# Layer 0 of a two-layer block: an interleaved opening, adaLN pieces of four k-tiles used two units behind their load, five granules, and the mixer's gate summed on PE

## The chip, the cores and the metric

The kernel runs on one core of a Trainium2 chip. The metric is the device time of one execution in microseconds. A core has five engines with an instruction stream of their own each: PE (matrix products), DVE and ACT (elementwise work), POOL (small work, and DMA issues of its own) and SP (which here only issues DMAs). Each stream is executed in order. Sixteen DMA engines carry all transfers.

## What is computed

Two layers over 256 tokens of width 2048, all in float32. Layer 0 has differential attention as its mixer, layer 1 a state-space mixer, and each has a gated feed-forward network (FFN). Cut to what matters here:

```python
c_act = jax.nn.silu(c)                              # 1 x 2048
for i in range(2):
    ada = c_act @ ada_w[i] + ada_b[i]               # 2048 x 12288
    shift1, scale1, gate1, shift2, scale2, gate2 = split(ada, 6)
    h = rms_norm(x, norm1_g[i]) * (1.0 + scale1) + shift1
    m = diff_attention(h, ...) if i == 0 else mamba2_ssd(h, ...)
    x = x + gate1 * m
    h = rms_norm(x, norm2_g[i]) * (1.0 + scale2) + shift2
    x = x + gate2 * swiglu(h, ffn_w_gate_up[i], ffn_w_down[i])
```

The adaLN vectors are products of one row with a large matrix: for layer 0 each of the six chunks is 2048 x 2048 weights, 16.8 MB, that are read once.

## The kernel before

**Weights and units.** Every weight matrix is read once, in units of 256 rows x 512 columns (0.524 MB), into a buffer `raw` of the pool `rawp` (seven buffers). ACT rounds it to `wh` (L268), DVE takes the rest `wl` (helper line L126), and PE multiplies: per unit two k-tiles x two token blocks x three products (`wh` by `ah`, `wl` by `ah`, `wh` by `al`), that is 12 products of 512 columns. Layer 0's input projection `da_w_in` is 96 units (12 blocks of columns, 8 units deep, the tuple `(n, half)`), its output projection `da_w_out` 32 units.

**The order of the work** is set when the program is written out. `push_unit` loads a unit and puts its products into a list, `fifo`; a unit's products are written when four more units have been pushed, so PE works four units behind the loads. `tick()`, once for each unit of products, also steps the generators of attention and lets adaLN jobs out at `ada["rate"]` jobs a unit.

**adaLN of layer 0** is computed in two ways. Shift and scale of the mixer come in *granules* of columns (`GRANULES`, six of them), laid out on the host by `lay_mods` as pieces of 128 partitions x 1024 (0.524 MB). A piece is used on PE: four products at a time with `cT32` (silu(c), each value repeated 32 times), in four column groups of the array, into bank `po` (shift) or `wk` (scale). `push_raw` puts a piece's use into the same `fifo`, so it comes up to four units behind its load. When a vector of a granule is done, ACT copies the sums (`adasb`), PE adds the four groups with `c32`, DVE makes `T0` and `S0`, and `modulate` makes the factors `ah`, `al` of these columns. The other vectors (mixer's gate `m0`, FFN's shift and scale `f0`) are *jobs* (`ada_job`): one row tile of 128 x 1024 is loaded and added up on DVE (`acc`). Shift and scale end in products with `ones` on PE, the gate in `partition_all_reduce` on POOL. The gate has 34 jobs, two of them for the bias.

**The opening.** `turn_x` takes the squares of x (ACT), `rstd` (POOL), scales x and turns it on PE into `xT`. The pieces of granule 0 follow. The small columns (`Columns`: norm gains and biases) and the rotary inputs come in through POOL's own queue; the buffer of `Columns` is one of `rawp`, and the rotary inputs lie in its rest.

**The input projection** goes through `order`: first every block's half 0, then deeper ones as granules become ready; partial sums that must leave PE's banks are put aside (`put_aside`, ACT copy or DVE addition). When a block of q or k is complete, its epilogue (normalising, rotary, transposes) runs as a generator, and behind it 12 attention steps (`attend`: four groups of heads x three), started at least four ticks apart. `until_output(g)` and `flush_steps` force the steps on when the output projection needs heads that are not there yet. `add_sums(ch)` adds a block of output to x with the gate; ahead of it `flush_jobs` writes out all jobs but the last 17, or all.

Of the kernel before, what the change touches and what calls it, by code (L numbers as in the profile page):

```python
# [20 lines left out]
D = 2048  # L21
# [24 lines left out]
GRANULES = [(0, 256), (256, 256), (512, 256), (768, 512), (1280, 512), (1792, 256)]  # L46
# [32 lines left out]
def lay_mods(w):  # L79

    import numpy as np

    parts = []
    for f, n in GRANULES:
        a = 1024 // n
        for v in range(2):
            m = w[:, v * D + f:v * D + f + n]
            parts.append(m.reshape(-1, a, 128, n).transpose(0, 2, 1, 3).reshape(-1))
    return np.ascontiguousarray(np.concatenate(parts)[None, :])
# [13 lines left out]
def block_kernel(ctx: ExitStack, tc: tile.TileContext, x, c, positions, norm1_g, norm2_g, ada_w, ada_b,  # L103
# [61 lines left out]
    waiting = {"u": 0, "a": 0}  # L165
    limit = {"u": W_BUFS, "a": 4}
# [42 lines left out]

    def tick():  # L210
# [12 lines left out]
        step_all()  # L223
# [60 lines left out]

    def push_raw(ap, fn):
# [4 lines left out]
        sp.dma_start(raw, ap)  # L290
        waiting["a"] += 1
        fifo.append(("a", lambda: fn(raw)))
# [86 lines left out]
    class Columns:  # L379


        def __init__(self, groups):

            self.groups = groups
            self.st = rawp.tile([128, 8, 128], F32, tag="raw", name="stage")
            for i, (_, aps) in enumerate(groups):
                r = 0
                for a in aps:
                    pool.dma_start(self.st[r:r + a.shape[0], i, :], a)
                    r += a.shape[0]  # L390

        def finish(self, i):
# [15 lines left out]
                     (bias_cols[1], [bias_rows[1, v:v + 2].rearrange("v k p -> (v k) p") for v in (0, 3)])])  # L408
    ps = bank("wk")
    pe.transpose(ps[:, :16], crows, ident[:16, :16])  # L410
    cT = const.tile([128, 16], F32, name="cT")
    act.activation(cT, ps[:, :16], AF.Silu)
# [277 lines left out]
    dp = pha.enter_context(tc.tile_pool(name="dp", bufs=1))  # L690
    cT32 = dp.tile([128, 512], F32, tag="on", name="cT32", bufs=1).rearrange("p (k m) -> p k m", m=32)
    dve.tensor_copy(cT32, cT[:, :, None].to_broadcast([128, 16, 32]))

    for b in range(2):
        sp.dma_start(xt[b], x[0, b * 128:(b + 1) * 128, :])
# [9 lines left out]
    lv = cols0.st[:, 4:6, :].rearrange("p a (i d) -> p (a i) d", d=64)  # L705
# [83 lines left out]
    def turn_x():  # L789

        junk = rowp.tile([128, D], F32, tag="gate", name="junk")
        rx = []
        for b in range(2):
            s = small(1, "ssum")
            act.activation(junk, xt[b], AF.Square, accum_out=s)
            rx.append(rstd_of(s, 1, D, "rstd"))
        for q in range(4):
            for b in range(2):
                xn = tmp("xn")
                if b:  # L800
                    dve.tensor_scalar(xn, xq[b][q], rx[b], None, op0=ALU.mult)
                else:
                    act.mul(xn, xq[b][q], rx[b])
                ps = bank("wk")
                for i in range(4):
                    pe.transpose(ps[:, i * 128:(i + 1) * 128], xn[:, i * 128:(i + 1) * 128], ident)
                dst = xT[q][:, :, b * 128:(b + 1) * 128]
                src = ps.rearrange("p (k t) -> p k t", k=4)
                if b:
                    act.copy(dst, src)  # L810
                else:
                    dve.tensor_copy(dst, src)

    def modulate(gi):

        f, n = GRANULES[gi]
        for k in range(f // 128, (f + n) // 128, 2):
# [11 lines left out]
            dve.tensor_tensor(l[:, k2, :], hm, h[:, k2, :].bitcast(F32), op=ALU.subtract)  # L829

    def granule(gi):

        f, n = GRANULES[gi]
        per = 1024 // n
        count = 16 // per
        sl = slice(f // 128, (f + n) // 128)
        nk = n // 128
        items = []

        def one(vec):  # L840
            st = {"held": []}

            def use(raw, u):
                if u == 0:
                    st["ps"] = bank(("po", "wk")[vec])
                st["held"] += [(u * per + a, raw[:, a * n:(a + 1) * n]) for a in range(per)]
                if len(st["held"]) < 4:
                    return
                for k, w in st["held"]:
                    g = k % 4  # L850
                    pe.matmul(st["ps"][32 * g:32 * g + 32, :n], cT32[:, k, :], w, start=(k < 4),
                              stop=(k >= 12), tile_position=(0, 32 * g), skip_group_check=True)
                st["held"] = []
                if u == count - 1:
                    st["sb"] = tmp("adasb")
                    act.copy(st["sb"][:, :n], st["ps"][:, :n])

            def finish():
# [8 lines left out]
            def push(u):  # L867
                at = f * 4096 + vec * n * D + u * 131072
                ap = bass.AP(tensor=ada_m.tensor, offset=ada_m.offset + at, ap=[[1024, 128], [1, 1024]])
                push_raw(ap, lambda raw: use(raw, u))  # L870
            for u in range(count):
                items.append(lambda u=u: push(u))
            return finish
        ends = [one(0), one(1)]
        return items, ends

# [191 lines left out]
    def put_aside(n):  # L1068

        bk = hold.pop(n)()  # L1070
# [12 lines left out]
    def push_step(n, half, first, last):  # L1083
# [5 lines left out]
        def run(u):  # L1089
            for b in range(2):  # L1090
                products(bk()[b], hq[q][b], half % 2, u, 512, first, last)
        push_unit(wi, half * 256, i * D + hg * 512, 512, run)
        if last:
            call(lambda: put_aside(n))

    split_at = 8
    order = [(n, 0) for n in range(split_at - 1, -1, -1)] + [(n, 0) for n in range(split_at, 12)]
    order += [(11, 1), (10, 1), (11, 2), (10, 2)]
    order += [(n, h) for n in range(9, split_at - 1, -1) for h in (1, 2)]
    order += [(n, h) for n in range(split_at - 2) for h in (1, 2)]  # L1100
    order += [(n, h) for n in (split_at - 2, split_at - 1) for h in (1, 2)]
    order += [(n, h) for n in range(split_at - 1, -1, -1) for h in (3, 4)]
    order += [(n, h) for n in range(split_at) for h in (5, 6, 7)]
    order += [(n, h) for n in range(split_at, 12) for h in (3, 4, 5, 6, 7)]
# [9 lines left out]

    made = [granule(gi) for gi in range(len(GRANULES))]

    def done_with(gi, vec):
        made[gi][1][vec]()
        if vec:
            modulate(gi)  # L1120

    turn_x()
    for k, it in enumerate(made[0][0]):
        it()
        if k == 5:
            def small_columns():
                for k in range(3):
                    cols0.finish(k)
                dve.tensor_scalar(subc, gcols[:, 64:65], 1.0 - LAMBDA_INIT, None, op0=ALU.mult)
            call(small_columns)  # L1130
# [5 lines left out]
    for gi in range(1, len(GRANULES)):  # L1136
        items = made[gi][0]
        for k, it in enumerate(items):
            ends = [(gi, k // (len(items) // 2))] if (k + 1) % (len(items) // 2) == 0 else []
            todo.append((it, ends))  # L1140
    late = deque()

    def ada_items(n):
        while late:
            call(late.popleft())
        for _ in range(n):
            if todo:
                it, ends = todo.popleft()
                it()
                for e in ends:  # L1150
                    late.append(lambda e=e: done_with(*e))

    call(lambda: done_with(0, 0))
    call(lambda: done_with(0, 1))
    open_ = set()
    pace = 0.0
    for at, (n, half) in enumerate(order):
        pace += 4 / 3 if at < 12 else 8 / 7
        ada_items(int(pace))
        pace -= int(pace)  # L1160
        if at == 16:
            call(lambda: active.append(rotary_tables()))
        if not todo and not late and not ada["rate"]:
            call(lambda: ada.update(rate=1.4))
            ada["rate"] = 1e-9
# [27 lines left out]
    def add_sums(ch):  # L1193
        flush_jobs(0 if ch == 2 else 17)
# [157 lines left out]
    def ssd_load():  # L1352
# [3 lines left out]
                                        ssd_ng[0].rearrange("(k p) -> k p", p=128)])])  # L1356
# [401 lines left out]
```

## Time and profile before

| | |
|---|---|
| median of 3 runs | 2791.36 us (2790.69 to 2792.46) |
| the profiled execution | 2787.28 us, span 2785.6 us |
| PE busy | 2665.7 us, 96% |
| DVE, ACT, POOL busy | 1936.5, 1314.9, 255.0 us |
| mean DMA rate | 246 GB/s |

Times in the profile count from the start of the span. A row of the timeline has start, length, engine, line, operation, output and inputs, and in brackets the idle time before it and what ended it. A fp32 product stands in the trace as two records, so counts there are double those of the program. Matrix products overlap in the pipeline, so their busy time isn't the time that each adds; that is read from the starts of neighbouring rows.

### The profile page before, as it was taken

How to read it: one execution, taken by the hardware profiler on the slowest of the kernel's cores; microseconds unless marked ns; L12 is line 12 of the kernel's file. 1: busy time of each engine (PE TensorE's matmuls, PEld its weight loads, DVE VectorE, ACT ScalarE, POOL GpSimd, SP SyncE). 2: the span in 40 equal slices, each digit the busy share in tenths (PEclk: the TensorE clock that was granted, in tenths of full speed). 3: DMA queues.
4: the chain of work that ended last, by engine and by line, in shares of the span. 5: the costliest groups of instructions: out<-in, count | busy, mean ns of one | idle time of the engine just before them, and what ended most of it. 6: DMA issues, size and time to landing. Idle time of an engine off the chain costs nothing.

```text
span 2785.6 us, 35877 instructions
## 1 busy us (share of the span) xinstructions
PE 2665.7 (96%) x13333; PEld 2207.0 (79%) x13333; DVE 1936.5 (70%) x2204; ACT 1314.9 (47%) x1844; POOL 255.0 (9%) x254
## 2 busy tenths in 40 slices
PE   3999889779999999999999999999999999999999
PEld 2666667658888888888899899888888888888887
DVE  1356999678878888677777877877664444445776
ACT  2433456445444444444655566564554444444443
POOL 2000424210211111000100001001000000000001
PEclk8999999889999999999999999999999999999999
DMA  4788877668899998788456666666645555556885
GB/s 167 264 306 296 284 272 266 235 240 289 316 336 353 338 330 318 260 289 296 147 193 219 224 226 216 236 218 211 220 155 188 194 189 190 189 188 211 292 289 184
DMA packets 188942, 684.56 MB, mean 246 GB/s; under 512 B 22224, under 2 KB 22528, under 8 KB 187488
## 3 DMA queue, kind: packets, MB, share of 16 engines
q1 hardware_dynamic: 186160, 678.59, 69.6%
q0 software_dynamic: 2176, 3.60, 0.4%
q8 instruction: 104, 1.70, 0.2%
q14 instruction: 70, 0.57, 0.1%
q10 hardware_dynamic: 432, 0.10, 0.0%
HBM read 680.00 MB, written 2.20 MB: 245 GB/s over the span
## 4 chain that ended last, share of the span: by engine, by line
PE 81%; DVE 7%; DMA 5%; ACT 3%; issue 2%; POOL 1%; ACTq 0%; SPq 0%; DVEq 0%; POOLq 0%
PE mm L126 65%; PE wk L126 13%; DMA raw<-in_da_w_in 4%; PE po L126 4%; DVE wl L126 2%; DVE acc L126 2%; ACT wh L268 1%; DMA raw<-in_da_w_out 1%; DVE mx L126 0%; DVE x L126 0%; POOL rq L432 0%; DVE partol L126 0%; ACT x L982 0%; DVE res L126 0%; DVE partoh L126 0%
## 5 line engine op out<-in xcount | busy, mean ns | idle before, releaser
L126 DVE TENSOR_TENSOR wl<-raw,wh 128x1024 fp32r<-128x1024 f32 (+1 forms) x888 | 1109.3, 1257 | 585.7 <-ACT wh L268 580.2
L268 ACT CAST wh<-raw 128x1024 fp32r<-128x1024 f32 (+1 forms) x888 | 926.0, 1046 | 1238.1 <-PE mm L126 720.3
L126 PE MATMUL mm<-wh,ah 128*128 128x512 f32 (+1 forms) x2560 | 1020.2, 399 | 4.5 <-ACT ah L828 4.1
L126 PE MATMUL mm<-wl,ah 128*128 128x512 f32 (+1 forms) x2560 | 1003.6, 392 | 0.0
L126 PE MATMUL mm<-wh,al 128*128 128x512 f32 (+1 forms) x2560 | 1003.3, 392 | 0.0
L126 PEld LDWEIGHTS mm<-wh,ah 128*128 128x128 f32 x2560 | 484.7, 189 | 128.4 <-issue 20.7
L126 PEld LDWEIGHTS mm<-wh,al 128*128 128x128 f32 x2560 | 484.4, 189 | 104.0 <-DVE al L126 1.5
L126 PEld LDWEIGHTS mm<-wl,ah 128*128 128x128 f32 x2560 | 484.7, 189 | 98.1 <-DVE wl L126 1.3
L126 DVE SCALAR_TENSOR_TENSOR acc<-raw,cT,acc 128x1024 f32<-128x1024 f32 x300 | 383.6, 1279 | 0.9
L532 POOL PARTITION_ALL_REDUCE gate<-acc x16 | 54.3, 3440 | 984.9 <-DVE acc L126 938.4
L126 PE MATMUL wk<-wh,ah 128*128 128x512 f32 x360 | 140.2, 389 | 0.0
L126 PE MATMUL wk<-wl,ah 128*128 128x512 f32 x360 | 140.1, 389 | 0.0
L126 PE MATMUL wk<-wh,al 128*128 128x512 f32 x360 | 140.1, 389 | 0.0
L126 PE MATMUL mm<-ah,wh 128*128 128x256 f32 x720 | 118.8, 285 | 0.0
L126 PE MATMUL mm<-al,wh 128*128 128x256 f32 x720 | 117.7, 283 | 0.0
L126 PE MATMUL mm<-ah,wl 128*128 128x256 f32 x720 | 117.7, 283 | 0.0
L126 PEld LDWEIGHTS mm<-ah,wh 128*128 128x128 f32 x720 | 100.2, 192 | 0.1
L126 PEld LDWEIGHTS mm<-ah,wl 128*128 128x128 f32 x720 | 100.2, 192 | 0.0
L126 PEld LDWEIGHTS mm<-al,wh 128*128 128x128 f32 x720 | 100.2, 192 | 0.0
L484 POOL PARTITION_ALL_REDUCE row<-acc x16 | 54.8, 3471 | 383.8 <-DVE acc L126 383.8
L126 PEld LDWEIGHTS wk<-wl,ah 128*128 128x128 f32 x360 | 67.6, 188 | 14.1 <-DVE wl L126 0.2
L126 PEld LDWEIGHTS wk<-wh,ah 128*128 128x128 f32 x360 | 67.6, 188 | 14.1
(295 smaller groups left out, 2039.6 us busy)
## 6 DMA issues: line engine op xcount, KB each, us to landing
raw<-in_ffn_w_gate_up SPq DMA_DIRECT2D x352, 512.0 KB, 4.4
raw<-in_ada_w SPq DMA_DIRECT2D x320, 512.0 KB, 5.1
raw<-in_ffn_w_down SPq DMA_DIRECT2D x176, 512.0 KB, 4.9
raw<-in_ssd_w_in SPq DMA_DIRECT2D x136, 512.0 KB, 4.6
raw<-in_da_w_in SPq DMA_DIRECT2D x96, 512.0 KB, 5.1
raw<-in_ada_m SPq DMA_DIRECT2D x64, 512.0 KB, 5.1
raw<-in_ssd_w_out SPq DMA_DIRECT2D x64, 512.0 KB, 4.3
raw<-in_da_w_out SPq DMA_DIRECT2D x32, 512.0 KB, 5.1
```

The source lines that it names most:

```text
L126: return fn(dst, *a, **k)
L268: act.copy(wh[:, :, :n], raw)
L484: pool.partition_all_reduce(row[:, o], acc[:, o], 128, ReduceOp.add)
L532: pool.partition_all_reduce(mods["G", key][:, o:o + 512], acc[:, i * 512:(i + 1) * 512], 128, ReduceOp.add)
```

## The change

It changes the stretch from the start of the program to the end of layer 0's output projection. Everything behind it is written out as before.

- **Opening.** The block squares are taken ahead of POOL's small transfers, block 0's ahead of silu(c) too. `turn_x(q)` works on one quarter, with all scaling on DVE and all copies on ACT; behind each quarter stand two of granule 0's eight pieces, of which six are loaded at once. `Columns` of layer 0 issues from ACT's queue into a tile of another pool, and the rotary inputs get a tile of their own.
- **Pieces.** All pieces are 256 columns x four k-tiles. `push_raw` no longer uses `fifo`: a piece's use is written two ticks behind its load (`LAG`), the finish one more tick behind. There are five granules (256, 256, 512, 512, 512 columns).
- **The gate** of the mixer is summed from 32 pieces on PE like shift and scale; a product with `c32m` (all 1/32) gives the sum in all partitions, and DVE adds it to `gate0`, in which the bias is loaded with one transfer.
- **Order.** Units stand in another order, with 1.5 pieces a unit, until all 96 pieces are through; from unit 56 on the 64 jobs of `f0` are let out at 1.1 a unit. `flush_jobs` stays ahead of the last `add_sums` alone.

```diff
-GRANULES = [(0, 256), (256, 256), (512, 256), (768, 512), (1280, 512), (1792, 256)]
+GRANULES = [(0, 256), (256, 256), (512, 512), (1024, 512), (1536, 512)]
+LAG = 2
...
     def tick():
+        for r in stream:
+            r[0] -= 1
+        while stream and stream[0][0] <= 0:
+            stream.popleft()[1]()
...
     def push_raw(ap, fn):
-        while waiting["a"] >= limit["a"]:
-            pop()
-        raw = rawp.tile([128, 2, 512], F32, tag="raw", name="raw").rearrange("p a n -> p (a n)")
-        load["dma"] += 1270.0
-        sp.dma_start(raw, ap)
-        waiting["a"] += 1
-        fifo.append(("a", lambda: fn(raw)))
+        while len(stream) > 3:
+            stream.popleft()[1]()
+        raw = load_raw(ap)
+        stream.append([LAG, lambda: fn(raw)])
...
+    def sums_of(vec, f, n, tag):
+        st, items = {}, []
+        def use(raw, sub, u):
+            if sub == 0 and u == 0:
+                st["ps"] = bank(tag)
+            o = sub * 256
+            for a in range(4):
+                k = 4 * u + a
+                pe.matmul(st["ps"][32 * a:32 * a + 32, o:o + 256], cT32[:, k, :], raw[:, a * 256:(a + 1) * 256],
+                          start=(u == 0), stop=(u == 3), tile_position=(0, 32 * a), skip_group_check=True)
+            if u == 3 and o + 256 == n:
+                st["sb"] = tmp("adasb")
+                act.copy(st["sb"][:, :n], st["ps"][:, :n])
...
+    def gate_items():
+        out_ = []
+        for ch in range(4):
+            st, items = sums_of(2, ch * 512, 512, "wk")
+            def finish(ch=ch, st=st):
+                ps2 = bank("wk")
+                pe.matmul(ps2, c32m, st["sb"], start=True, stop=True)
+                o = slice(ch * 512, ch * 512 + 512)
+                dve.tensor_tensor(gate0[:, o], gate0[:, o], ps2, op=ALU.add)
...
+    for q in range(4):
+        turn_x(q)
+        for i in (2 * q, 2 * q + 1):
+            first[i][0][1](raws[i])
...
-    ada_job(0, 2, fin_gate("m0"), gate=True)
...
+    for gi, n in ((1, 10), (2, 2), (3, 8), (4, 12)):
+        todo.extend(granule(gi))
+        todo.extend(gates[:n])
+        del gates[:n]
...
-        pace += 4 / 3 if at < 12 else 8 / 7
+        pace += 1.5
...
-            call(lambda: ada.update(rate=1.4))
+            call(lambda: ada.update(rate=1.1))
...
     def add_sums(ch):
-        flush_jobs(0 if ch == 2 else 17)
+        if ch == 2:
+            flush_jobs()
```

What stands on POOL in the opening, before: the last transfers for the rotary tables (`stage`), the masks of attention (`negm`), then the two blocks' `rstd`.

```order
L707 DMA stage<-in_da_lambda_q 128x64
L707 DMA stage<-in_da_lambda_k 128x64
L775 MEMSET negm_150 128x512
L778 AFFINE_SELECT negm_150<-negm_150 128x128 x4
L775 MEMSET negm_164 128x512
L778 AFFINE_SELECT negm_164<-negm_164 128x128 x2
L431 TENSOR_SCALAR rstd<-ssum 128x1
L432 TENSOR_TENSOR rstd<-rstd,neghalf 128x1
```

And with the change, from the identity matrix `ident` on:

```order
masks.py:199 AFFINE_SELECT ident<-ident 128x128
L422 MEMSET ones 128x1
L424 MEMSET neghalf 128x16
L426 MEMSET c_105 128x1
L435 TENSOR_SCALAR rstd<-ssum 128x1
L436 TENSOR_TENSOR rstd<-rstd,neghalf 128x1
L435 TENSOR_SCALAR rstd<-ssum 128x1
L436 TENSOR_TENSOR rstd<-rstd,neghalf 128x1
L713 MEMSET c32m 128x128
L716 DMA posi<-in_positions 128x2x1
```

Both `rstd` moved ahead of all of POOL's transfers and masks, and the seven `stage` loads left POOL's queue.

SP's loads from the start of the program on, before (`in_ada_m` are the pieces, `in_da_w_in` the units):

```order
L403 DMA crows<-in_c 16x128
L695 DMA x_103<-in_x 128x2048
L695 DMA x_104<-in_x 128x2048
L290 DMA raw<-in_ada_m 128x1024 x9
L264 DMA raw<-in_da_w_in 128x1024
L290 DMA raw<-in_ada_m 128x1024
L264 DMA raw<-in_da_w_in 128x1024
```

And with the change:

```order
L696 DMA x_100<-in_x 128x2048
L292 DMA raw<-in_ada_m 128x1024 x8
L1144 DMA gate<-in_ada_b 128x2048
L292 DMA raw<-in_ada_m 128x1024
L269 DMA raw<-in_da_w_in 128x1024
L292 DMA raw<-in_ada_m 128x1024 x2
L269 DMA raw<-in_da_w_in 128x1024
```

The gate's bias stands behind the first eight pieces, and two and one pieces alternate ahead of the units, up to the 58th unit.

PE at the start of the output projection, where forced attention steps stand between units (`oh`, `ol` are the halves of a head group's output; `negm` with `identb` and `kT` by `qT` are the scores of a step, `x` its probabilities, `partv` its values, `on` an output). Between the second and the third unit, before:

```order
L126 MATMUL mm<-wh,ol 128x512
L126 MATMUL po<-partv,x_104 128x128 x4
L126 MATMUL mm<-wh,oh 128x512
L126 MATMUL mm<-wl,oh 128x512
L126 MATMUL mm<-wh,ol 128x512
```

And at that place with the change:

```order
L125 MATMUL wk<-ident,partol 128x128 x4
L125 LDWEIGHTS identb
L125 MATMUL wk<-negm_179,identb 128x512
L125 LDWEIGHTS identb
L125 MATMUL wk<-negm_179,identb 128x512
L125 MATMUL wk<-kT,qT 128x256 x4
L125 MATMUL po<-partv,x_100 128x128 x4
L125 MATMUL wk<-ident,on 128x128 x4
L125 MATMUL wk<-ident,x_100 128x128 x4
L125 MATMUL mm<-wh,oh 128x512
```

A step's scores and another step's probabilities moved to this place, from between the last units of the input projection.

More of the change, by code (lines that the diff above doesn't have):

```diff
@@ L164, in block_kernel @@
     lagging = []
-    waiting = {"u": 0, "a": 0}
-    limit = {"u": W_BUFS, "a": 4}
+    waiting = {"u": 0}
+    limit = {"u": W_BUFS}
     jobs = deque()
@@ L379, in block_kernel, with __init__ @@
     class Columns:
[L382 removed]
+        def __init__(self, groups, st, queue):
             self.groups = groups
[L385 removed]
+            self.st = st
             for i, (_, aps) in enumerate(groups):
@@ L407, in block_kernel @@
                      (bias_cols[0], [bias_rows[0, v:v + 2].rearrange("v k p -> (v k) p") for v in (0, 3)]),
[L408 to L412, printed above, removed]
+                     (bias_cols[1], [bias_rows[1, v:v + 2].rearrange("v k p -> (v k) p") for v in (0, 3)])],
+                    actp.tile([128, 8, 128], F32, tag="ah", name="stage"), act)
     xt = [const.tile([128, D], F32, name=f"x_{b}") for b in range(2)]
@@ L787, in block_kernel, with turn_x @@
     whole, hq = {}, {}
-    def turn_x():
-        junk = rowp.tile([128, D], F32, tag="gate", name="junk")
-        rx = []
+    def turn_x(q):
         for b in range(2):
[L794 to L812, printed above, removed]
+            xn = tmp("xn")
+            dve.tensor_scalar(xn, xq[b][q], rx[b], None, op0=ALU.mult)
+            ps = bank("wk")
+            for i in range(4):
+                pe.transpose(ps[:, i * 128:(i + 1) * 128], xn[:, i * 128:(i + 1) * 128], ident)
+            act.copy(xT[q][:, :, b * 128:(b + 1) * 128], ps.rearrange("p (k t) -> p k t", k=4))
     def modulate(gi):
@@ L829, in modulate, with item, finish @@
             dve.tensor_tensor(l[:, k2, :], hm, h[:, k2, :].bitcast(F32), op=ALU.subtract)
+            made_halves.add(k // 2)
+    made_halves = set()
+    def item(vec, f, u):
+        at = ((vec * 8 + f // 256) * 4 + u) * 131072
+        return bass.AP(tensor=ada_m.tensor, offset=ada_m.offset + at, ap=[[1024, 128], [1, 1024]])
+    def sums_of(vec, f, n, tag):
[11 more added lines that the diff above has]
+                act.copy(st["sb"][:, :n], st["ps"][:, :n])
+        for sub in range(n // 256):
+            for u in range(4):
+                items.append((item(vec, f + 256 * sub, u), lambda raw, sub=sub, u=u: use(raw, sub, u)))
+        return st, items
     def granule(gi):
         f, n = GRANULES[gi]
-        per = 1024 // n
-        count = 16 // per
         sl = slice(f // 128, (f + n) // 128)
         nk = n // 128
[L838 to L858, printed above, removed]
+        out_ = []
+        for vec in range(2):
+            st, items = sums_of(vec, f, n, ("po", "wk")[vec])
+            def finish(vec=vec, st=st):
                 ps2 = bank("wk")
@@ L865, in finish @@
                     dve.scalar_tensor_tensor(t[:, sl], t[:, sl], 1.0, n1c[0][:, sl], op0=ALU.add, op1=ALU.mult)
[L867 to L875, printed above, removed]
+                    modulate(gi)
+            out_ += [(it, None) for it in items[:-1]] + [(items[-1], finish)]
+        return out_
+    def gate_items():
+        out_ = []
+        for ch in range(4):
[5 more added lines that the diff above has]
+                dve.tensor_tensor(gate0[:, o], gate0[:, o], ps2, op=ALU.add)
+            out_ += [(it, None) for it in items[:-1]] + [(items[-1], finish)]
+        return out_
     oT = [[] for _ in range(4)]
```

112 lines of the change are left out of this document (59 added, 53 removed).

## The prediction

> **What bounds the kernel now.** I read the page's totals first, then the span cut into the stages of layer 0's mixer, then the opening instruction by instruction, then the waits inside the stages.
>
> ```profile
> span 2785.6 us, 35877 instructions
> PE 2665.7 (96%) x13333; PEld 2207.0 (79%) x13333; DVE 1936.5 (70%) x2204; ACT 1314.9 (47%) x1844; POOL 255.0 (9%) x254
> ```
>
> ```profile
> core 0: us, PE busy (x) PEld busy (x) DVE busy (x) ACT busy (x) POOL busy (x), PEclk, DMA share, GB/s
> 0.00:65.70 65.70, 19.13 (x116) 10.97 (x116) 9.12 (x22) 14.67 (x20) 14.76 (x39) 0.88 0.46 164
> 65.70:287.60 221.90, 212.77 (x1076) 147.94 (x1076) 119.55 (x196) 81.92 (x104) 3.89 (x4) 0.97 0.81 288
> 287.60:460.70 173.10, 149.72 (x742) 117.69 (x740) 162.38 (x238) 85.81 (x199) 70.34 (x76) 0.94 0.80 277
> 460.70:524.90 64.20, 50.51 (x270) 39.56 (x269) 49.11 (x84) 40.04 (x124) 15.89 (x26) 0.89 0.59 191
> 524.90:616.80 91.90, 72.85 (x266) 55.47 (x267) 72.55 (x64) 29.90 (x39) 16.47 (x10) 0.85 0.83 298
> 634.90:2785.60 2150.70, 2143.08 (x10780) 1821.12 (x10777) 1511.40 (x1575) 1048.05 (x1325) 132.11 (x97) 1.00 0.69 242
> ```
>
> From 634.9 us on PE is busy 2143.08 of 2150.70 us, and both programs issue the same PE instructions there. So the change is decided before: five stages with 112 us of idle PE. In the table the first two columns are the stage and its length, then the busy time of each engine with its count of instructions, the granted clock, the share of the DMA engines and their rate. I call the stages A (opening, to the first weight product at 65.7), B (units 1 to 59 of the input projection; a unit is 12 products of 512 columns), C (units 60 to 96, DVE busy 94%), D (units 97 to 105, attention runs out), E (units 106 to 127 of the output projection).
>
> **A, the opening.**
>
> ```profile
> 9.90 0.28 POOL masks.py:199 TENSOR_SCALAR_AFFINE_SELECT ident<-ident 128x128 f32<-128x128 f32 x1 [8.90 <-issue]
> 12.66 1.91 ACT L795 ACTIVATE junk<-x 128x2048 f32<-128x2048 f32 x1
> 19.32 0.56 POOL L707 DMA_DIRECT2D stage<-in_da_lambda_q  x1
> 24.54 0.60 POOL L432 TENSOR_TENSOR rstd<-rstd,neghalf 128x1 f32<-128x1 f32 x1
> 25.94 1.11 PE L126 MATMUL wk<-ident,xn 128*128 128x128 f32 x4 [15.43 <-ACT xn L803]
> 43.58 3.62 PE L126 MATMUL po<-raw,cT 128*32 128x256 f32 x32
> ```
>
> ```profile
> SPq L290 <- PE po L126: 39.5, 5, 34.7
> ```
>
> ```profile
> L695 SPq DMA_DIRECT2D x<-in_x x2: 406/415/424, 1.3 to 1.7; - x2
> ...
> DMA to landing us min/median/max: 4.9/6.0/7.0
> ```
>
> ```profile
> 65.71 5.42 PE mm L126 x12
> ...
> 635.14 38.14 PE mm L126 x168
> ```
>
> The squares of x end at 12.66+1.91 = 14.6, but rstd comes at 24.5, behind POOL's list of small transfers and masks; the turning of x follows, and the adaLN pieces only at 43.58. SP, whose raw buffers are all full, stands 34.7 us in one wait for them, and the DMA engines stand with it:
>
> ```profile
> 0.00:20.00 20.00, 0.28 (x1) 0.18 (x1) 0.56 (x2) 5.36 (x6) 9.20 (x25) 1.00 0.71 268
> 20.00:40.00 20.00, 6.63 (x24) 4.29 (x24) 3.25 (x6) 4.21 (x7) 5.56 (x15) 1.00 0.08 7
> ```
>
> So nothing of the 24 us between rstd and the pieces is a limit of a resource; it is an order. Now rstd stands before POOL's transfers. ident still comes at 10.2; x lands 4.9 to 7.0 us after issue, so block 0's square is done before ident and block 1's near 12.8; rstd of block 1 near 13.8, first pair of transposes done near 15.4. Then PE has, without rival: three more quarters at 2 x 1.11 = 2.2, eight pieces at 3.62/4 = 0.9 each, 1 us for the small columns: 15.4+6.6+7.2+1 = 30. Behind them stand four pieces of granule 1 (3.6) and the finish of T and S (1.0): 35; then DVE and ACT (three low parts, modulation, cast) add some 5. First product near 40 (36 to 45) against 65.7: **minus 25.7**. The seven stage loads moved to ACT cost seven issues ahead of x's square, hidden while x is in flight and ident is not there; without that cover they would cost the 3 us of their issue. SP's second half of x and its first pieces now wait for earlier transfers' completion counters, which ACT's seven share; these are small or (x's first half) land by 6.2, and PE wants the first piece only at 15. POOL's ten transfers for rotary and lambda now start near 14 us and are used from the third unit on; at 0.56 us each they are all out by 21, some 25 us ahead of that use. rstd of both blocks, both scalings (now all on DVE, 0.5 us each) and both copies (all on ACT) lie in the chain already counted. For both ends of the range: 36 if PE's pieces cost half, as later in the trace; 45 if the fourth piece of granule 1, whose buffer is freed only by the opening's last pieces, lands 5 us behind them.
>
> **B.** A unit costs PE 12 x 38.14/168 = 2.72 us. For the piece:
>
> ```profile
> 222.46 1.07 PE L126 MATMUL wk<-raw,cT 128*32 128x512 f32 x8
> 223.34 0.61 PE L126 MATMUL po<-raw,cT 128*32 128x256 f32 x8
> 228.81 1.05 PE L126 MATMUL wk<-c,adasb 128*128 128x1 f32 x8 [1.87 <-ACT adasb L856]
> ```
>
> Two pieces take 223.34-222.46 = 0.88 us, say 0.5 each with what stands between; a finish 0.5 to 1.0. Before: 59 x 2.72 + 55 x 0.5 + 7 = 195 us of PE work in 221.9 us (of 64 pieces, nine lie ahead of the first unit). After, B also holds the gate's 32 pieces, and twelve of 96 lie ahead: 59 x 2.72 + 84 x 0.5 + 6.5 for finishes + 4 for the four products with c32m (no row has one; eight 128-column fp32 products take 1.05 us below, so 0.5 to 1 us each) = 213 us. Its transfers rise from 2.2 to 2.5 loads a unit: some 139 loads of 0.524 MB after the first product, 73 MB.
>
> ```profile
> 800.00:900.00 100.00, 100.00 (x456) 82.73 (x455) 85.03 (x76) 45.38 (x49) 16.35 (x8) 1.00 0.94 344
> ```
>
> At the 344 GB/s of this row 73 MB take 212 us, at the 288 of stage B 253. I take 230, midway: the PE sum with 8% on it, where the old stage had 14%, since a piece now holds its buffer for two units, not four, and stage lies in another pool, so seven raw buffers serve instead of six. B ends near 270 (249 to 298) against 287.6: **the lead shrinks to 17.6**. Six more pairs of partial sums are added on DVE (12 x 0.68 = 8 us), hidden: DVE is busy 120 of 222 us; uncovered they would hold PE's banks. The rotary tables' small DVE work, fourteen units earlier, is hidden by the same slack. The new wait here is PE's for a piece two units behind its load: behind it in PE's order stand that unit's successor and, through the bank, ACT's copy adasb and the finish; behind ACT's copy stand the casts of the next units. One late piece thus stops both streams, which is the second rival. The gate's 1 MB bias transfer on SP (3 us at 344 GB/s) is hidden behind the opening's PE work.
>
> **C.** DVE is the bound.
>
> ```profile
> L126 DVE SCALAR_TENSOR_TENSOR acc<-raw,cT,acc 128x1024 f32<-128x1024 f32 x51 | 65.3, 1280 | 0.5
> L126 DVE TENSOR_TENSOR wl<-raw,wh 128x1024 fp32r<-128x1024 f32 x37 | 45.4, 1226 | 1.4 <-ACT wh L268 1.4
> L126 DVE TENSOR_REDUCE mx<-wk 128x2 f32<-128x512 f32 (+1 forms) x15 | 10.2, 683 | 1.6 <-PE wk L126 1.6
> ```
>
> ```profile
> 287.60:460.70 173.10, 5.70 (x48) 5.66 (x48) 67.19 (x54) 0.00 (x0) 0.94 0.80 277
> ...
> 524.90:616.80 91.90, 0.00 (x0) 0.00 (x0) 28.28 (x21) 13.16 (x4) 0.85 0.83 298
> ```
>
> The second fence is the tile acc alone. Its 54 instructions in C become 37 x 1.1 = 41, 13 x 1.28 = 16.6 us less; attention begins six units later (first scores behind unit 72, not 66), so two of its twelve steps leave C, some 5 us. DVE falls from 162 to 141; at 94% that is 150 us, a gain of 23. PE's own work is about 130, so little is late next; What shares the gain is PE's order. I take **18** (5 to 23), nearer the upper row, for chains of attention that wait in PE's order.
>
> **D.** What left C comes here: the output projection needs heads that are not done, and PE walks through attention alone, DVE, ACT and POOL each in turn on one head's data.
>
> ```profile
> 486.89 1.05 PE L126 MATMUL po<-partv,x 128*128 128x128 f32 x8
> ...
> 491.42 2.08 PE L126 MATMUL wk<-kT,qT 64*128 64x256 f32 x8
> 497.88 2.08 PE L126 MATMUL po<-partv,x 128*128 128x128 f32 x8 [4.39 <-ACT on L1043]
> ...
> 502.68 1.13 PE L126 MATMUL wk<-kT,qT 64*128 64x256 f32 x8
> ```
>
> From scores to next scores a forced round lasts 502.68-491.42 = 11.3 us. The order shows one to two rounds more (behind units 98 and 100): **plus 16** (5 to 23). The same product takes 1.05 us at 486.89, and 2.08 after 4.39 us of idleness. The Trainium skill (TensorE: Matmul & The Clock Gate, "Why this matters for your kernels") says that an idle gap above some 3 us drops PE's clock; the trace agrees. By it warm rounds would be 1 to 2 us shorter and the term 14; the measured round holds the cold clock.
>
> **E.**
>
> ```profile
> PE mm L126 <- DVE res L126: 7.8, 1, 7.8
> PE mm L126 <- DVE wl L126: 5.9, 6, 2.4
> PE mm L126 <- ACT wh L268: 5.4, 2, 4.0
> ```
>
> These are PE's waits in E, in all, how often, and the longest. E's 23 units need 62.6 us and take 91.9. The residual stands behind the flushed gate jobs on DVE (21 of acc, 28.28 us) and four all-reduces on POOL. After, 32 shift and scale jobs of each kind at 1.1 a unit from the 57th end near unit 115, nothing is flushed, and the gate is there since unit 57. The transfers fall from 298 GB/s x 91.9 us = 27 MB to some 36 loads, 19 MB, 55 us at 344: no bound. 62.6 plus 7 of remaining waits: **minus 22** (27 if these go too; 12 if the waits for casts and low parts, 11.3 us, stay).
>
> The gate itself, by parts: 34 loads become 32 pieces and one bias transfer, about the same bytes; 34 instructions on DVE (43 us, counted in C and E) become four additions of 0.68 and four copies on ACT; 13.16 us of POOL go; PE gains the 32 x 0.5 + 4 us counted in B.
>
> **The sum.** 17.6+18-16+22 = 41.6 us off the profiled execution, whose 2787.28 us (span 2785.6) lie 4.1 below the median of 2791.36. Taken off the median: 2750.
>
> **The rivals.** First, B's transfers stay at 288 GB/s: 40+253 = 293, the lead there is lost, in all 41.6-23 = 18.6: 2773. For it: a low part waiting for its transfer holds up the sums behind it on DVE, and with them PE's banks, as before; against: the rate of 344 came through the same raw pool, and the old pieces held their buffers for four units.
>
> Second, slower: two units are too short, and PE stands at each piece for its transfer.
>
> ```profile
> raw<-in_ada_m SPq DMA_DIRECT2D x64, 512.0 KB, 5.1
> ```
>
> With one landing of 5.1 us for each of 59 steps B takes 301 instead of 230: 2821. It is slower from 230+41.6 = 272 us, 4.6 a step instead of 3.9. Against it: two units are 7.4 us with their pieces, longer than 5.1.
>
> Third, the reordered opening doesn't do what it says: PE still waits for transfers queued behind x, the first product comes at 52, 12 us later: 2762. For it: x and eight pieces are 6.3 MB, all asked for at once; against: in the old opening 268 GB/s x 20 us = 5.4 MB of the same transfers were through by 20 us.
>
> Fourth, three more rounds in D (34 us) and no gain in C: 41.6-18-18 = 5.6: 2786, no change.
>
> **Chances.** Forecast 0.63, first 0.15, third 0.07, fourth 0.06, second 0.09. So faster by over 0.2% (5.6 us, what a measurement tells from no change) 0.85, same 0.06, slower 0.09. The range 2722 to 2781 holds the forecast with most of its ends, the first and the third; the fourth, the second and the joint far ends (2708, 2807) stay out.
>
> **What would show it.** First unit near 40 us; unit 59's end near 270 with a rate of 310 to 345 GB/s; 64 instead of 98 acc instructions before the FFN and no all-reduce of the gate there; C near 155, D near 80, E near 70 us. Wrong: PE waits for raw<-in_ada_m all through B, or a D beyond 100 us.

## The result and the profile after

The changed kernel takes 2749.8 us (median; 2745.9 to 2751.04) against 2791.03 us (2790.1 to 2792.46) for the kernel before, beside it on the same chip: a ratio of 0.9849, 95% interval 0.9832 to 0.9867, so 41.2 us less. Its profiled execution took 2745.9 us, 3.9 below its median; that of before lay 4.1 below its own. Differences between the two profiles can therefore be set against differences of medians. One of the six executions of e1_gate_back below took 5349.81 us for a reason that stays open; its median there includes it (2771.1 without), its ratio does not.

The totals of the changed kernel's page:

```profile
PE 2671.9 (97%) x13725; PEld 2207.1 (80%) x13725; DVE 1898.9 (69%) x2183; ACT 1318.5 (48%) x1847; POOL 240.1 (9%) x244
```

PE has 392 instructions more, DVE 21 and POOL 10 fewer. The stages A to E, cut at the same units as before, and the rest of the kernel (columns as in the prediction: stage, length, busy time of PE, PE's weight loads, DVE, ACT and POOL, granted clock, share of the DMA engines, GB/s):

```profile
0.00:42.30 42.30, 17.36 (x141) 9.05 (x141) 9.64 (x23) 16.75 (x23) 11.96 (x33) 0.82 0.92 338
42.30:278.50 236.20, 230.36 (x1444) 154.70 (x1445) 119.51 (x199) 83.82 (x104) 0.00 (x0) 0.99 0.88 318
278.50:427.30 148.80, 137.90 (x677) 109.46 (x675) 140.57 (x206) 80.59 (x174) 69.33 (x69) 0.94 0.78 270
427.30:509.90 82.60, 61.28 (x314) 46.16 (x314) 49.55 (x97) 44.82 (x149) 24.49 (x40) 0.83 0.38 124
509.90:576.00 66.10, 64.29 (x285) 52.56 (x284) 55.37 (x57) 30.18 (x39) 1.09 (x2) 0.97 0.89 339
594.10:2743.90 2149.80, 2143.08 (x10780) 1821.00 (x10778) 1511.92 (x1575) 1047.90 (x1325) 131.77 (x97) 1.00 0.69 243
```

The last row says that nearly everything is decided before the FFN: 2149.8 against 2150.7 us behind it. The FFN's first unit starts at 594.1 instead of 634.9, 40.8 us earlier.

The opening of the changed kernel, from PE's timeline (start, duration, instruction; in brackets what PE idled for):

```profile
11.45 1.12 PE L125 MATMUL wk<-ident,xn 128*128 128x128 f32 x4 [1.43 <-DVE xn L125]
...
23.25 1.07 PE L125 MATMUL wk<-raw,cT 128*32 128x256 f32 x16
29.23 1.08 PE L125 MATMUL po<-raw,cT 128*32 128x256 f32 x8 [4.91 <-DMA raw<-in_ada_m]
...
35.40 1.08 PE L125 MATMUL po<-raw,cT 128*32 128x256 f32 x8 [1.38 <-DMA raw<-in_ada_m]
36.41 1.87 PE L125 MATMUL wk<-c,adasb 128*128 128x1 f32 x8
42.26 0.80 PE L125 MATMUL mm<-wh,ah 128*128 128x512 f32 x1 [3.98 <-ACT ah L831]
```

The first quarter of x turns at 11.45 instead of 25.94. Granule 0's eight pieces are through at 24.3, but its finish stands in PE's order behind four pieces of granule 1, whose transfers land up to 35.4. PE waits 7.8 us for these four. So the new end of the opening is set by where the finish stands, and there by the landings of pieces that it does not need: 24.3 was possible, 36.4 is what it got.

PE's waits in B (what PE waited for, us in all, times, longest), then in E. The wait of 4.0 us for `ah` ends at 42.26 with the first product, as the last row above shows, so it belongs to A; 5.8 us are left for B:

```profile
PE wk L125 <- ACT adasb L855: 4.0, 6, 0.7
PE mm L125 <- ACT ah L831: 4.0, 1, 4.0
PE mm L125 <- DVE partol L125: 1.8, 1, 1.8
...
PE mm L125 <- ACT wh L273: 1.1, 1, 1.1
PE mm L125 <- DVE wl L125: 0.8, 1, 0.8
```

No wait for raw<-in_ada_m in B: PE never stands at a piece for its transfer, and the second rival falls with this view alone. In E 1.9 us of waits are left of the 19.1 listed in the prediction.

### The profile page after: what moved, and what is told of

It is laid out like the page before. It is cut to its first block, busy times and chain, and to the rows that moved or that the text cites. A ratio compares the mean times of both kernels' runs of the same rounds, so it can differ in the third digit from the quotient of the medians.

```text
span 2743.9 us, 36630 instructions
## 1 busy us (share of the span) xinstructions
PE 2671.9 (97%) x13725; PEld 2207.1 (80%) x13725; DVE 1898.9 (69%) x2183; ACT 1318.5 (48%) x1847; POOL 240.1 (9%) x244
## 3 DMA queue, kind: packets, MB, share of 16 engines
q1 hardware_dynamic: 186016, 678.59, 70.2%
q8 instruction: 107, 1.75, 0.3%
## 4 chain that ended last, share of the span: by engine, by line
PE 90%; DVE 4%; ACT 2%; issue 2%; POOL 1%; DMA 1%; SPq 0%; ACTq 0%; DVEq 0%; POOLq 0%
PE mm L125 72%; PE wk L125 14%; PE po L125 4%; DVE wl L125 1%; DVE acc L125 1%; ACT x L1000 1%; DMA raw<-in_ada_m 0%; DVE mx L125 0%; DVE x L125 0%; DVE partoh L125 0%; ACT wh L273 0%; POOL rq L436 0%; DVE qss L125 0%; DMA raw<-in_da_w_in 0%; POOL rq L435 0%
## 5 line engine op out<-in xcount | busy, mean ns | idle before, releaser
L125 DVE SCALAR_TENSOR_TENSOR acc<-raw,cT,acc 128x1024 f32<-128x1024 f32 x270 | 345.2, 1279 | 0.1
L536 POOL PARTITION_ALL_REDUCE gate<-acc x12 | 41.1, 3469 | 931.0 <-DVE acc L125 924.1
```

The source lines that it names most:

```text
L125: return fn(dst, *a, **k)
L536: pool.partition_all_reduce(mods["G", key][:, o:o + 512], acc[:, i * 512:(i + 1) * 512], 128, ReduceOp.add)
```

## The experiments

Every run was timed beside the kernel before, on the same chip. The columns A to E are stage lengths in us, from the one profiled execution, cut at the same units. That execution is not always near the median: the changed kernel's is 3.9 us and e8's 9.5 us below it, e2's 4.0 above. Stages B and E of unchanged code differ by 2 to 4 us between executions, with the granted clock; differences of that size are not read.

| run | median us | ratio to before (95%) | A | B | C | D | E |
|---|---|---|---|---|---|---|---|
| before | 2791.0 | 1 | 65.7 | 221.9 | 173.1 | 64.2 | 91.9 |
| changed kernel | 2749.8 | 0.9849 (0.9832–0.9867) | 42.3 | 236.2 | 148.8 | 82.6 | 66.1 |
| e1_gate_back | 2771.2 | 0.9922 (0.9909–0.9936) | 39.1 | 213.6 | 176.5 | 80.5 | 91.6 |
| e2_rstd_late | 2754.3 | 0.9867 (0.9853–0.9880) | 47.8 | 240.3 | 149.3 | 82.2 | 68.7 |
| e3_lag1 | 2744.5 | 0.9834 (0.9820–0.9848) | 44.3 | 232.6 | 151.9 | 80.2 | 66.2 |
| e4_pace3 | 2750.0 | 0.9851 (0.9838–0.9863) | 42.3 | 237.0 | 164.9 | 70.2 | 66.9 |
| e5_open2 | 2735.3 | 0.9802 (0.9789–0.9815) | 28.3 | 236.9 | 149.7 | 81.7 | 68.3 |
| e6_mirror | 2730.9 | 0.9789 (0.9775–0.9802) | 43.4 | 236.1 | 149.7 | 64.6 | 66.7 |
| e7_group3 | 2760.0 | 0.9894 (0.9880–0.9907) | 48.5 | 240.8 | 149.1 | 82.2 | 68.2 |
| e8_combo | 2733.0 | 0.9799 (0.9786–0.9812) | 29.2 | 241.9 | 152.1 | 64.6 | 66.2 |
| e9_open2_mirror | 2720.2 | 0.9749 (0.9736–0.9762) | 30.0 | 237.9 | 149.2 | 64.7 | 66.5 |
| e10_early4 | 2709.3 | 0.9707 (0.9694–0.9721) | 29.7 | 238.9 | 147.6 | 55.9 | 68.2 |
| e11_jobs_late | 2759.3 | 0.9883 (0.9867–0.9900) | 42.7 | 236.6 | 139.0 | 79.6 | 90.4 |

The theory behind them is the prediction's: the opening is a chain of order, C is bounded by DVE, D by a late start of attention, E by work that stood ahead of the residual, and B pays for the gate. The main rival is that stages only hand time on to one another.

**e1_gate_back: the gate back to DVE and POOL.**

```
-    sp.dma_start(gate0, bcast(ada_b[0, 2 * D:3 * D], D))
...
-    gates = gate_items()
+    ada_job(0, 2, fin_gate("m0"), gate=True)
+
+    gates = []
...
-        pace += 1.5
+        pace += 4 / 3 if at < 12 else 8 / 7
...
-        if at == 56:
-            call(lambda: ada.update(rate=1.1))
+        if not todo and not ada["rate"]:
+            call(lambda: ada.update(rate=1.4))
+            ada["rate"] = 1e-9
...
-        if ch == 2:
-            flush_jobs()
+        flush_jobs(0 if ch == 2 else 17)
```

> The changed kernel with one part undone: the gate of the mixer is made again by 34 jobs on DVE and four all-reduces on POOL, its 32 pieces and its 1 MB bias transfer leave PE's stream, and the paces of the pieces (4/3, then 8/7 a unit) and of the jobs (1.4 once the pieces are through) are those of before. Theory (the gate's move pays in the stages C and E, and costs in B): first product 3 us earlier (39, without the bias transfer), B some 236-32x0.65-5 = 210 us, C back to some 170, E back to 90: about 2749.8-3-26+22+24 = 2767, between 2760 and 2785. Rival (the opening and the new order of the pieces give the gain, and the jobs of the gate would fit into DVE's idle time of B and D now that attention starts later): 2740 to 2753, with C near 150 and E near 70.

B, C and E of this run:

```profile
39.10:252.70 213.60, 209.77 (x1189) 147.35 (x1189) 124.12 (x201) 79.02 (x99) 0.00 (x0) 0.99 0.82 293
252.70:429.20 176.50, 146.24 (x692) 116.03 (x691) 161.62 (x226) 83.00 (x176) 67.07 (x69) 0.91 0.81 277
509.70:601.30 91.60, 71.34 (x270) 53.84 (x269) 72.62 (x64) 31.03 (x43) 19.54 (x13) 0.91 0.84 296
```

The theory holds: 21.4 us slower than the changed kernel, with C longer by 27.7 and E by 25.5, B shorter by 22.6 and A by 3.2. D, 80.5, stays long without the gate on PE. DVE's 161.62 us in C and 72.62 in E are those of the kernel before (162.38 and 72.55). So the gate's move, with the paces and the flush that go with it, is worth about half of the 41 us, and what it costs is in B: 22.6 us for 32 pieces and four finishes.

**e2_rstd_late: the scale of x again behind POOL's list.**

```
-        rx.append(rstd_of(s, 1, D, "rstd"))
+        rx.append(s)
...
+    rx = [rstd_of(s, 1, D, "rstd") for s in rx]
     first = granule(0)
```

> The changed kernel with POOL's part of the scale of x put back behind POOL's transfers and masks, as before; nothing else is touched. Theory (a chain of small instructions sets the opening, and what is lost there is lost to the end): rstd comes some 10 us later, PE's first pieces with it, first product at 50 to 53 instead of 42.3, time 2758 to 2761. Rival (the opening is now bounded by its transfers, whose share of the DMA engines is 0.92 up to 42 us, so PE's order there matters little): first product at 43 to 45, time 2750 to 2752. A third case: the first product comes later, but B, busy with transfers that have landed meanwhile, takes it back: 2750 to 2754 with B shorter.

PE's timeline of this run:

```profile
22.74 2.32 PE L125 MATMUL wk<-ident,xn 128*128 128x128 f32 x8 [12.78 <-DVE xn L125]
...
42.06 1.87 PE L125 MATMUL wk<-c,adasb 128*128 128x1 f32 x8
47.83 0.80 PE L125 MATMUL mm<-wh,ah 128*128 128x512 f32 x1 [3.90 <-ACT ah L831]
```

The turning begins 11.3 us later, the finish comes 5.7 us later, the first product 5.6: half is absorbed, since the pieces of granule 1, for which PE waited before, have landed meanwhile. The medians differ by 4.5 us, about what the first product lost. Neither the theory nor the rivals had this case (B is not shorter); order and transfers share the opening.

**e3_lag1: pieces taken up one unit behind their load.** `LAG = 2` becomes `LAG = 1`.

> The changed kernel with the pieces taken up one unit behind their load instead of two. Theory (a landing of about 5 us is longer than a unit with its pieces, 3.9 us, and shorter than two): PE waits for raw<-in_ada_m at each step of B, some 1 us or more each, B 60 us longer: 2790 to 2815. Rival (PE's queue runs behind the loads by more than a unit anyway, since SP issues loads as soon as buffers come free): no waits for raw<-in_ada_m, 2748 to 2752.

The theory fails: nothing in PE's waits in B names raw<-in_ada_m, and the ratio's interval overlaps that of the changed kernel (the median lies 3.5 us below the rival's range). The likely reason, the rival's, is that the lag alone does not say how early a piece is loaded: in the program's order the loads stand four units (W_BUFS) ahead of PE. No run varies that distance.

**e4_pace3: steps of attention three ticks apart.** `PACE = 4` becomes `PACE = 3`.

> The changed kernel with one number changed: steps of attention may follow one another three ticks apart instead of four. Theory (D is long because attention starts late and its last steps run alone on PE): attention ends a quarter sooner, so D falls from 82.6 to about 65, and C rises by some 5 to 10, DVE being at 94% there: 2738 to 2746. Rival (the steps are bound by the chain of DVE, ACT and POOL within a step, or by DVE's work in C, so that asking for them sooner only makes PE wait in C for what it waits for in D): C and D together the same, 2747 to 2753.

C and D of this run:

```profile
279.30:444.20 164.90, 148.88 (x721) 117.80 (x721) 148.63 (x234) 87.41 (x200) 72.91 (x79) 0.92 0.73 246
444.20:514.40 70.20, 53.17 (x273) 41.57 (x272) 39.44 (x69) 38.77 (x124) 19.41 (x29) 0.85 0.43 141
```

The rival holds: D falls by 12.4, C grows by 16.1, and the time stays. Eleven us of PE's busy time come to C, and the stage grows by five more.

**e5_open2: the finish at once, the gate's bias later.**

```
-    sp.dma_start(gate0, bcast(ada_b[0, 2 * D:3 * D], D))
 ...
-            call(finish)
+            finish()
 ...
-        pace += 1.5
+        pace += 0.75 if at < 4 else 1.6
 ...
+        if at == 6:
+            sp.dma_start(gate0, bcast(ada_b[0, 2 * D:3 * D], D))
```

> The changed kernel with its opening ordered once more: granule 0 is finished as soon as its eight pieces are through, not behind four pieces of granule 1; the 1 MB bias of the gate is loaded between the seventh and the eighth unit instead of ahead of the first; the pieces of the first four units come at 0.75 a unit and then at 1.6 instead of 1.5 throughout. Theory (PE's order, not the transfers, sets the first product: finish at 26 instead of 36, then the same 5.9 us to the first product): first product at 32 to 34 instead of 42.3; B takes four more pieces, 4x0.65 = 2.6 us, and carries the rest on: 2741 to 2745. Rival (the opening is bounded by its transfers, whose share was 0.92 up to 42 us: what PE begins earlier it waits for in B): first product earlier, but B longer by as much, 2747 to 2752.

```profile
24.25 1.17 PE L125 MATMUL wk<-c,adasb 128*128 128x1 f32 x8
28.30 0.80 PE L125 MATMUL mm<-wh,ah 128*128 128x512 f32 x1 [2.89 <-ACT wh L273]
...
28.30:265.20 236.90, 231.31 (x1477) 156.44 (x1478) 122.41 (x202) 87.12 (x108) 0.00 (x0) 0.99 0.92 343
```

The first two lines are PE's timeline, the third is stage B. The first product comes at 28.3, sooner than the theory's 32, and B keeps its length although it holds four more pieces: 14.5 us less in the medians. So the landings that held the changed kernel's first product were a matter of order: what stood ahead of the finish. In B the rate rises to 343 GB/s, and PE waits once for a piece, 1.0 us. The run makes three edits at once (the finish, the bias, the pace of the first four units), and their shares are not separated; in e1, without the bias transfer, A was 3.2 us shorter.

**e6_mirror: the blocks of the first heads whole four units earlier.**

```
-    order += [(n, h) for n in range(A) for h in (4, 5)]
-    order += [(n, h) for n in (A - 1, A - 2) for h in (6, 7)]
-    order += [(n, h) for n in range(A - 2) for h in (6, 7)]
+    order += [(n, h) for n in range(A - 1, -1, -1) for h in (4, 5)]
+    order += [(n, h) for n in (0, 1) for h in (6, 7)]
+    order += [(n, h) for n in range(2, A) for h in (6, 7)]
```

(The loops over halves 1, 2 and 3 are turned round likewise.)

> The changed kernel with the same units in a mirrored order within the input projection, so that the blocks of the first heads (queries and keys of head group 0) are whole at units 58 and 60 instead of 62 and 64; the number of partial sums is the same. First scores stand four units earlier in PE's order (behind unit 68 instead of 72). Theory (D is long because attention starts late): D falls by 4 units' time, some 10 us, from 82.6 to about 72, C stays below 155: 2738 to 2744. Rival (as with the faster pace of attention's steps: what comes earlier lies in C, where DVE is busy 140.6 of 148.8 us, and C grows by what D loses): C+D stays within 3 us of 231, 2747 to 2753.

```profile
279.50:429.20 149.70, 139.58 (x714) 110.95 (x713) 144.72 (x226) 85.79 (x199) 80.74 (x83) 0.97 0.78 266
429.20:493.80 64.60, 50.54 (x276) 38.39 (x276) 44.48 (x78) 38.49 (x122) 14.88 (x26) 0.92 0.52 165
```

D falls by 18.0 us to what it was in the kernel before (64.2), C grows by 0.9, and the rival is out. The theory had the direction and too small an amount. Attention begun earlier is worth more than the four units' own 11 us: 38 of PE's instructions leave D (314 to 276) with 10.7 us of its busy time, and come to C (677 to 714), where busy time grows by 1.7. In e4 the same steps were only packed more densely behind an unchanged start.

**e7_group3: three pieces every second unit.**

```
-        pace += 1.5
+        pace += 3.0 if at % 2 == 0 else 0.0
```

> The changed kernel with the pieces taken up three at a time every second unit instead of one and two in turn; their number, their work and the order of the units are the same. It measures how the price of a piece on PE divides. In the timeline of B a unit with one piece takes 3.5 us from start to start, with two 4.0, without 2.7. Theory (each change from weight products to pieces costs PE some 0.3 us by itself, beside 0.5 for the piece): 28 changes fewer, B shorter by 8 us, 228 instead of 236, and 2741 to 2744. Rival (the price is in the pieces, 0.65 us each, or three pieces at once make PE wait for transfers or casts): B 234 to 242, 2747 to 2755.

How the price of a piece divides is read from the last weight product ahead of the pieces to the first one behind them: one and two pieces in the changed kernel, three in this run:

```profile
140.21 0.39 PE L125 MATMUL mm<-wh,al 128*128 128x512 f32 x1
140.52 0.64 PE L125 MATMUL po<-raw,cT 128*32 128x256 f32 x8
141.09 0.50 PE L125 MATMUL mm<-wh,ah 128*128 128x512 f32 x1
...
143.73 0.39 PE L125 MATMUL mm<-wh,al 128*128 128x512 f32 x1
144.04 1.07 PE L125 MATMUL po<-raw,cT 128*32 128x256 f32 x16
145.04 0.50 PE L125 MATMUL mm<-wh,ah 128*128 128x512 f32 x1
```

```profile
142.93 0.39 PE L125 MATMUL mm<-wh,al 128*128 128x512 f32 x1
143.25 1.50 PE L125 MATMUL po<-raw,cT 128*32 128x256 f32 x24
144.68 0.50 PE L125 MATMUL mm<-wh,ah 128*128 128x512 f32 x1
```

The distances are 0.88, 1.31 and 1.75 us: 0.43 to 0.44 for each piece more. Products alone follow one another every 0.23 us, and the second product behind pieces comes after 0.34 or 0.35, 0.11 late. One piece thus costs 0.88-0.23+0.11 = 0.76, two 1.19, three 1.63, which is 0.44 a piece and 0.32 for each change to pieces and back. The theory's split is shown; its sum is not. The run is 10.2 us slower, outside both ranges:

```profile
48.50:289.30 240.80, 229.41 (x1425) 160.38 (x1426) 118.77 (x198) 82.89 (x104) 0.00 (x0) 0.96 0.84 305
PE wk L125 <- ACT adasb L855: 11.0, 10, 1.8
```

Six pieces of granule 1, not four, and a part of its finish now stand ahead of the first unit, and A is 6.2 us longer. In B the nine us saved are lost to waits for the finish's copy on ACT (11.0 instead of 4.0) and, as an estimate, to a granted clock of 0.96 instead of 0.99, 3% of 240 us. Why the clock is lower is not settled.

**e8_combo: e5's opening, e6's order and pieces by three.**

> The three edits together: the finish of granule 0 at once and the bias of the gate later, the mirrored order of units, and the pieces three at a time every second unit, from the fifth unit on. If each theory holds: 6.5+8+8 = 22 us less, about 2727. If only the opening's: 2741 to 2745. If none: 2747 to 2753.

2733.0 (2723.5 to 2736.1), with a B of 241.9, the longest of all. It fits none of the three cases; beside the next run, which differs in the pace of the pieces alone, it loses 12.8 us, nearly half of the 29.6 that the other two edits bring. Its stages, from the fastest of its executions, show 5.7 of them:

**e9_open2_mirror: e5 and e6 together.**

> The second opening and the mirrored order of units together, with the pieces one by one as in the changed kernel (0.75 a unit for the first four, then 1.6). Theory (the two gains lie in different stages, A and D, and add up): 2749.8-14.5-18.9 = 2716, between 2712 and 2721. Rival (an earlier opening makes the later stages wait for transfers, or lowers the granted clock, as with pieces by three): 2724 to 2735, with B or C longer than in either alone.

2720.2: within 4 us of the sum of the two gains. They lie in different stages and add up, and the rival is out.

**e10_early4: attention four more units earlier.** The edits of e9 stand in it; of the order only the lines that are new beside e9 are shown.

```
+    order += [(n, h) for n in range(A - 1, 3, -1) for h in (4, 5)]
+    order += [(n, h) for n in range(4) for h in (4, 5, 6, 7)]
+    order += [(n, h) for n in range(4, A) for h in (6, 7)]
 ...
-    for gi, n in ((1, 10), (2, 2), (3, 8), (4, 12)):
+    for gi, n in ((1, 10), (2, 2), (3, 4), (4, 16)):
```

> As the run before it, and besides the units ordered so that the first four blocks are made whole one after the other (halves 4 to 7 in one accumulation, four partial sums of a pair fewer on DVE), with four pieces of the gate put behind the last granule so that this granule is through in time. First scores stand four units earlier in PE's order again (about 50 rows). Theory (attention's start still sets D: 64.6 us against 50.5 of PE's busy time): D down to 52 to 56, 2704 to 2712. Rival (DVE, busy 144.7 of 149.7 us in C, is the bound, so that attention begun earlier only makes C longer): C and D together as before, 2712 to 2721.

```profile
268.60:416.20 147.60, 139.26 (x732) 110.65 (x731) 144.81 (x226) 88.55 (x217) 64.34 (x77) 0.99 0.81 272
416.20:472.10 55.90, 48.08 (x251) 37.06 (x250) 39.58 (x67) 33.11 (x100) 12.77 (x19) 0.91 0.58 185
```

The theory's numbers hold: D is 55.9, C no longer. The edit also saves partial sums on DVE, so the earlier start is not isolated here as it is in e6. At 2709.3 us (2706.08 to 2711.36) this version beats both kernels: 81 us or 2.9% below the kernel before, and 40 below the changed one.

**e11_jobs_late: DVE's jobs for the FFN begun 20 units later.**

```
-        if at == 56:
-            call(lambda: ada.update(rate=1.1))
+        if at == 76:
+            call(lambda: ada.update(rate=1.5))
```

> The changed kernel with its 64 remaining jobs of DVE (shift and scale for the layer's FFN, acc of 1.28 us each) begun 20 units later, behind unit 76 instead of 56, and at 1.5 a unit instead of 1.1, so that they still end before the FFN. Some 22 of them, 28 us of DVE's work, leave stage C. Theory (DVE is the bound of C, 140.6 busy of 148.8 us): C falls towards PE's own 138, to 139 to 143, and part of it is kept at the end: 2739 to 2746. Rival (C is as much PE's as DVE's, 137.9 us busy, and D or E now wait for the jobs): C within 3 us of 149, or D and E longer by what C loses, 2747 to 2760.

```profile
279.30:418.30 139.00, 130.77 (x661) 104.24 (x659) 123.47 (x190) 80.39 (x174) 58.57 (x69) 0.99 0.69 230
...
497.90:588.30 90.40, 74.91 (x301) 60.03 (x300) 71.17 (x72) 32.54 (x44) 5.99 (x8) 0.87 0.88 323
```

```profile
PE wk L125 <- DVE acc L125: 8.8, 2, 7.9
PE mm L125 <- DVE res L125: 4.1, 1, 4.1
```

Both halves of the picture in one run. Of the `acc` instructions 14 leave C (18 us of DVE's work; 22 were expected), and C falls by 9.8 us to 139.0: the load on DVE made it longer. Only 2.7 of the 9.8 are PE's waits (10.9 us in all in the changed kernel's C, 8.2 here). The other 7.1 are PE's busy time, 130.77 instead of 137.90 us, at a granted clock of 0.99 instead of 0.94. E grows by 24.3 to 90.4, as long as before the change, with PE waiting for jobs and for the residual behind them (the second fence: PE's waits in E). DVE's 71.17 us there are near the old 72.55. The rival's total is right; of the theory the fall of C is right, and nothing of it is kept at the end.

## Why the prediction was right

The predicted sum of -41.6 us stands against -40.8 in the profiles and -41.2 in the medians. By its terms:

- **A, -25.7 predicted, -23.4 measured.** The mechanism (an order, not a resource) is shown by e2 for the scale of x, with half of its delay absorbed, and by e5 for the finish. Granule 0 was to be through at 30 and was at 24.3: the price of the pieces was high (0.9 each; from 17.56 on two take 1.07). From there to the first product 10 us were allowed, and it took 18.0: the wait for the landings of granule 1's pieces, 7.8 us, stood only in the far end of the range, 45. The two errors nearly cancel, which is luck. That a finish 12 us earlier was to be had was not seen. (The "24 us between rstd and the pieces" of the kernel before are 19.0, from 24.54 to 43.58; no sum rests on them.)
- **B, +8 predicted (230), +14.3 measured (236.2).** The step that was mis-sized is "say 0.5 each with what stands between": a piece alone costs 0.76, two 1.19, so 1.95/3 = 0.65 each at this pace. What was left out is the change between products and pieces, 0.32 us each time. 84 pieces make 54.6 instead of 42 us, and the PE sum 225.6 instead of 213, with finishes and gate products as predicted. The waits in B, 5.8 us, and the first unit, which took 5.2 us (42.26 to 47.42) instead of 2.7, bring it to 233.8; the last 2.4 us are not assigned. The margin of 17 us (8%) was reasoned from transfers, and PE waited for no piece: it stood in for part of these costs, so that 230 is nearer than its reasons. The rate stayed at 318 GB/s, and it was not at its limit: with e5 it is 343.
- **C, -18 predicted, -24.3 measured.** DVE's busy time came out at 140.57 (predicted 141), and the stage is 148.8, DVE at 94% again. The upper row, -23, was right; the five us withheld for attention in PE's order were not needed. e1 and e11 show from both sides that C follows DVE's load (161.62 us busy in 176.5, 123.47 in 139.0). That DVE alone bounds it is not shown: in e11 most of the gain is PE's own busy time, at a higher granted clock, and PE is then as full (130.77 of 139.0 us) as DVE was.
- **D, +16 predicted, +18.4 measured.** The reason, attention's later start, is shown by e6, which gives the 18.0 back by the order of units alone; the gate's pieces are not the cause, since D is 80.5 without them in e1.
- **E, -22 predicted, -25.8 measured.** The floor was miscounted: units 106 to 127 are 22, not 23 (264 products in the trace), so 62.6 should be 59.8, and 2.7 of the 3.8 us by which E beat the forecast are this unit. Of the waits, 7 us were allowed to remain and 1.9 did; the other 4.4 us of the stage, PE's other work and its clock (0.97), stood in no term. e1 brings the old E back (91.6), and e11 does so with other jobs.

So A and D came out 4.7 us worse than forecast, B 6.2 worse, C and E 10.1 better; that the sum fits to a us is luck. That each stage moved the way forecast is not, though B moved nearly twice as far as forecast. No rival is needed: the first is excluded by B's rate (318 GB/s) and length (236.2, not 253), the second by the waits and by e3, the third by A, the fourth by C.

## What to carry to other kernels

A stage is worth moving work into only while its own bound has room, and what is moved must be priced at the place it lands: the gate left DVE's tight stages C and E for 53 us and paid 23 on PE in B; with A and D the two profiles differ by 25 us, the medians by 21. What sets a later stage can be an earlier choice of order: which blocks become whole first cost 18 us in D, and packing the late work more densely (e4) did not get that back. After an opening is reordered, look at what stands between its last input and its first product; here a finish queued behind work that nobody needed yet held 14 us.

## What the runs showed of the hardware

A change from products of 512 columns to pieces 32 columns wide and back costs PE 0.32 us by itself, beside 0.44 for each piece (e7's 0.88, 1.31 and 1.75 us).

The granted clock in the profile's rows does not always show PE's speed. In e2, after 12.78 us of idleness, eight transposes took 2.32 us at 22.74 and eight more 1.09 at 30.01, while the granted clock stood at 1.00 in both stretches:

```profile
30.01 1.09 PE L125 MATMUL wk<-ident,xn 128*128 128x128 f32 x8
...
22.70:28.70 6.00, 5.87 (x32) 3.60 (x32) 2.25 (x5) 1.76 (x3) 0.59 (x2) 1.00 0.23 77
30.00:36.00 6.00, 5.11 (x63) 3.22 (x59) 1.50 (x6) 2.69 (x6) 0.00 (x0) 1.00 1.00 403
```

The Trainium skill (TensorE: Matmul & The Clock Gate, "Why this matters for your kernels") has an idle gap drop PE's clock; the trace agrees, but the column of the granted clock doesn't show it here. In the changed kernel it does: after waits of 4.91 and 3.98 us the first twelve products take 5.1 us instead of 2.72, and the granted clock of that stretch is 0.51:

```profile
42.26:47.40 5.14, 5.14 (x12) 4.01 (x13) 1.80 (x2) 0.00 (x0) 0.00 (x0) 0.51 0.62 234
```

The transfers reach more than the 344 GB/s on which the prediction's lower end for B rested: 403 GB/s over the 6 us of e2's last line above. Over the whole of B the highest is e5's 343.
